# A two-layer attention trunk: the softmax weights transposed by block transposes on VectorE and DMAs through DRAM instead of by TensorE

## The chip, the cores and the metric

The kernel runs on one core of a Trainium2 chip. The metric is the device time of one execution in microseconds (us), as the median of several runs. Single executions were also profiled; all rows below come from one such execution of the kernel before.

## The reference

The reference takes 256 tokens of width 2048 through two layers. Each layer normalises its input (RMSNorm), projects it by one wide matrix to queries, keys, values and a gate, applies rotary embedding to queries and keys, does attention per head, multiplies by silu(gate), projects back and adds the result to the input. A last RMSNorm ends it. Everything is float32.

```
layer 0:  ya = dilated attention, 8 heads of 128   (three windows merge into one softmax with a fixed mask)
          yb = (softmax(q1 k1') - lam * softmax(q2 k2')) v,  4 heads with v of width 256
          x  = x + (concat(ya, rmsnorm(yb)) * silu(z)) @ w_out
layer 1:  yc = causal softmax attention, 16 heads of 128  (one block of 256 keys, so no block choice remains)
          x  = x + (yc * silu(z)) @ w_out
out = rmsnorm(x)
```

Scores are causal: query tokens 0 to 127 see keys 0 to 127, query tokens 128 to 255 see all 256 keys. So a head's softmax weights are three blocks of 128 x 128.

## The kernel before

**Precision.** Float32 products are made of two parts: a high part rounded to the type `float32r`, and a low part, the rest. A product is high x high + high x low + low x high (`mm3`). ScalarE writes the high part as a copy, VectorE subtracts it from the source for the low part.

**Weights.** The weights stream through SBUF in pieces of 128 x 2048 (1 MB, tile `raw`, three buffers, issued by SyncE). Each piece is split in two halves of 128 x 1024 by `split`: ScalarE writes `wh` (L133), VectorE writes `wl` (L134). There are four buffers of `wh` and `wl`, and `split` is called three halves ahead of use.

**Slots.** The main loop walks over slots. A slot is half of one 128 x 1024 split, and two slots use up one split. Weights come in chunks: for each layer four groups g, each with q, k, z (two chunks of 8 slots each) and v (16 slots; group 0 has v first), then four output chunks of 16 slots. In a slot of a q, k or z chunk TensorE does four pairs of matmuls, one with `wh` against the high and low input (L529, 512 columns) and one with `wl` against the high input (L531, 256 columns). After a slot's matmuls the loop calls what `at(slot, f, ...)` has put down for it. Layer 1 begins at slot 320, its output chunks at slot 576.

**Attention.** When the second k chunk of a group has ended, at slot `nxt`, the attention of the group is put down slot by slot. In groups 0 and 1 of layer 0 and in all groups of layer 1 there are four heads h:

- `attn_s` at `nxt + 1 + 3h`: scores by TensorE (`softmax`, tile `ps_s`), masked maximum by VectorE, exponential by ScalarE, scaling by VectorE; the result is tile `p`, 128 x 384, the three blocks side by side, query by key.
- `attn_t` at `nxt + 6 + 3h`: three TensorE transposes of `p` into PSUM (`ps_t`, L352), then the split of the transposed weights: `th` (ScalarE, L357) and `tl` (VectorE, L358), both for the first two blocks, and `t` (ScalarE, L362), a plain copy of the third.
- `attn_o` at `base + 2 + 2h`, `base` being `nxt + 16` for g = 0 and `nxt + 32` otherwise: the product with v (`po`; three matmuls in `mm3`, two with `t`), and `finish_y`, which multiplies by the gate `u` and splits the result (`y`, `yh`, `yl`).

Groups 2 and 3 of layer 0 hold two differential heads each: `diff_s` twice a head, `attn_t` with all three blocks split (`both`), `diff_o` at `nxt + 34 + 5h` (with a square root on GpSimd, tile `rb`, L201), `diff_y` at `nxt + 38 + 5h`.

**Order.** Every engine works through its instructions in a fixed order. The order on each engine is not that of the program text: a planner goes through the program with costs of its own and places an instruction on its engine once, by its account, its inputs and its buffer are there, with the earlier written ones first. It also sets all semaphores. SyncE issues the weights and the outputs, ScalarE the load `gf`, GpSimd no DMA; GpSimd has six small `pow` operations of `rsqrt_mean` and two at the end.

Of the kernel before, what the change touches and what calls it, by code (L numbers as in the profile page):

```python
# [8 lines left out]
F32 = mybir.dt.float32  # L9
F32R = mybir.dt.float32r  # L10
AF = mybir.ActivationFunctionType
# [4 lines left out]
P = 128  # L16
S = 256
# [38 lines left out]
def trunk(ctx, tc, x_nat, x_t, w0, o0, w1, o1, g0, g1, gfin, lam, subln, cos_t, sin_t,  # L56
          mask_d, mask_c, ident_in, out):
    nc = tc.nc
# [8 lines left out]
    work = ctx.enter_context(tc.tile_pool(name="work", bufs=1))  # L67
    small = ctx.enter_context(tc.tile_pool(name="small", bufs=1))
    pacc = ctx.enter_context(tc.tile_pool(name="pacc", bufs=2, space=PSUM))
    patt = ctx.enter_context(tc.tile_pool(name="patt", bufs=1, space=PSUM))  # L70


    chunks = [(kind, layer, g, j, w) for layer in range(2) for kind, g, j, w in layer_chunks()]
# [37 lines left out]
    def split(m):  # L111
        if m >= 2 * NR:
            return
        load(m // 2)
        r = raws[m // 2][:, 2 * (m % 2) * CW:2 * (m % 2 + 1) * CW]
        last = m - 2 * NR + 8
        if 0 <= last < 4:
            h = [xhl[2 * last + i].rearrange("p a b -> p (a b)") for i in range(2)]
            lo = [xhl[8 + 2 * last + i].rearrange("p a b -> p (a b)") for i in range(2)]
        else:  # L120
            ht = wpool.tile([P, 2 * CW], F32R, tag="wh", name=f"wh{m}")
            lt = wpool.tile([P, 2 * CW], F32R, tag="wl", name=f"wl{m}")
            w = wide[m // 2]
            h, lo = ([t[:, i:i + w] for i in range(0, 2 * CW, w)] for t in (ht, lt))
        if m < 2 or 0 <= last < 4:
            for i in range(2):
                if m == 0:
                    split_x(0, i, xr(i))
                rr = r[:, i * CW:(i + 1) * CW]
                nc.scalar.activation(h[i], rr, AF.Copy)  # L130
                nc.vector.tensor_sub(lo[i], rr, h[i].bitcast(F32))
        else:
            nc.scalar.activation(ht, r, AF.Copy)  # L133
            nc.vector.tensor_sub(lt, r, ht.bitcast(F32))  # L134
        splits[m] = (h, lo)
# [18 lines left out]
    def xr(kt):  # L154
        return xraw[kt // 4][:, kt % 4]
# [3 lines left out]
    def split_x(layer, kt, src):  # L159
        g = g_sb[:, layer, kt:kt + 1]  # L160
        h, lo = xhl[kt][:, 0], xhl[kt][:, 1]
        x_ins.append(nc.scalar.activation(h, src, AF.Copy, scale=g).ins)
        nc.vector.scalar_tensor_tensor(lo, src, g, h.bitcast(F32), op0=ALU.mult, op1=ALU.subtract)
# [6 lines left out]
    ident = const.tile([P, P], F32, name="ident")  # L170
# [85 lines left out]
    def at(slot, f, *a):  # L256
        fill.setdefault(slot, []).append((f, a))
# [52 lines left out]
    def mm3(out_, lh, ll, rh, rl, start=True, stop=True):  # L310
        for i, (l, r) in enumerate(((lh, rh), (lh, rl), (ll, rh))):
            nc.tensor.matmul(out_, l, r, start=start and i == 0, stop=stop and i == 2)  # L312

    def softmax(layer, g, h, mask):
        (q, qh, ql), (k, kh, kl) = Q[layer, g], K[layer, g]
        ps = patt.tile([P, 3 * P], F32, tag="S", name="ps_s", bufs=2)
        nc.tensor.matmul(ps[:, 0:P], q[:, h, 0:P], k[:, h, 0:P], start=True, stop=True)  # L317
        mm3(ps[:, P:3 * P], qh[:, h], ql[:, h], kh[:, h], kl[:, h])
        st = small.tile([P, 3, 2], F32, tag="st", name="st", bufs=4)
        p = work.tile([P, 3 * P], F32, tag="p", name="p", bufs=3)  # L320
        for i, sl in enumerate((slice(0, P), slice(P, 3 * P))):
            nc.vector.tensor_tensor_reduce(out=p[:, sl], in0=ps[:, sl], in1=mask[:, sl], scale=-SCALE,  # L322
                                           scalar=3.0e38, op0=ALU.add, op1=ALU.min,
                                           accum_out=st[:, 0, i:i + 1])
        for i, sl in enumerate((slice(0, P), slice(P, 3 * P))):
            nc.scalar.activation(p[:, sl], p[:, sl], AF.Exp, bias=st[:, 0, i:i + 1], scale=-1.0,  # L326
                                 accum_out=st[:, 1, i:i + 1])
        nc.vector.reciprocal(st[:, 2], st[:, 1])
        return p, st
# [16 lines left out]
                                               op0=ALU.mult, op1=ALU.add)  # L346
            box["p"] = p

    def attn_t(box, both=False):
        pt = patt.tile([P, 3 * P], F32, tag="T", name="ps_t")  # L350
        for i in range(3):
            nc.tensor.transpose(pt[:, i * P:(i + 1) * P], box["p"][:, i * P:(i + 1) * P], ident)  # L352

        n = 3 * P if both else S
        th = work.tile([P, n], F32R, tag="th", name="th", bufs=4)
        tl = work.tile([P, n], F32R, tag="tl", name="tl", bufs=4)
        nc.scalar.activation(th, pt[:, 0:n], AF.Copy)  # L357
        nc.vector.tensor_sub(tl, pt[:, 0:n], th.bitcast(F32))  # L358
        t = None
        if not both:  # L360
            t = work.tile([P, P], F32, tag="t", name="t", bufs=4)
            nc.scalar.activation(t, pt[:, n:3 * P], AF.Copy)  # L362
        box["t"] = (t, th, tl)

    def y_tiles():
# [139 lines left out]
    for (kind, layer, g, j, w), slot0 in list(zip(chunks, starts))[:-1]:  # L505
        ps = pacc.tile([P, 2, CW], F32, tag="acc", name=f"acc{slot0}")
        per = CW // w
        nxt = slot0 + KT // per
        for slot in range(slot0, nxt):
            if slot % 2 == 0:  # L510
                split(slot // 2 + AHEAD)
                load((slot // 2 + AHEAD) // 2 + 1)
            if layer == 0 and slot < KT and 2 * AHEAD <= slot + 4 < KT:
                split_x(0, slot + 4, xr(slot + 4))
            wh, wl = splits[slot // 2]
            for i in range(per):
                kt = (slot - slot0) * per + i
                ww = (slot % 2) * per + i
                first, final = kt == 0, kt == KT - 1
                for b in range(2):  # L520
                    bs = slice(b * P, (b + 1) * P)
                    if w == CW:
                        a_h, a_l = (yh[kt][:, bs], yl[kt][:, bs]) if kind == "o" else \
                            (xhl[kt][:, 0, bs], xhl[kt][:, 1, bs])
                        mm3(ps[:, b], a_h, a_l, wh[ww], wl[ww], start=first, stop=final)
                    else:

                        xx = xhl[kt].rearrange("p a b -> p (a b)")
                        nc.tensor.matmul(ps[:, b], wh[ww][:, bs], xx, start=first, stop=False,  # L529
                                         skip_group_check=True)  # L530
                        nc.tensor.matmul(ps[:, b, 0:S], wl[ww][:, bs], xx[:, 0:S], start=False, stop=final,  # L531
                                         skip_group_check=True)
            for f, a in fill.pop(slot, []):
                f(*a)
        if kind == "z":
            evac_z(ps, layer, g, j)
        elif kind == "q":
            evac_rope(ps, "q", Q, layer, g, j)
        elif kind == "k":
            evac_rope(ps, "k", K, layer, g, j)  # L540
            if j == 0:
                continue
            if layer == 0 and g >= 2:
                for h in range(2):
                    box = {}
                    at(nxt + 1 + 6 * h, diff_s, layer, g, h, box, 0)
                    at(nxt + 3 + 6 * h, diff_s, layer, g, h, box, 1)
                    at(nxt + 8 + 6 * h, attn_t, box, True)
                    at(nxt + 34 + 5 * h, diff_o, layer, g, h, box)
                    at(nxt + 38 + 5 * h, diff_y, layer, g, h, box)  # L550
            else:
                for h in range(4):
                    box = {}
                    base = nxt + (16 if g == 0 else 32)
                    at(nxt + 1 + 3 * h, attn_s, layer, g, h, md if layer == 0 else mc, box)
                    at(nxt + 6 + 3 * h, attn_t, box)
                    at(base + 2 + 2 * h, attn_o, layer, g, h, box)
        elif kind == "v":
            if slot0 == 0:
                at(nxt + 5, evac_v, ps, layer, g)  # L560
            else:
                evac_v(ps, layer, g)
        else:
            evac_o(ps, layer, g)
            if layer == 0:
                at(nxt + 3, next_x, g, 0)
                at(nxt + 6, next_x, g, 1)
            else:
                at(nxt + 4, times_g, g)
# [65 lines left out]
```

## Time and profile before

| | us |
|---|---|
| median of 3 runs | 958.21 (958.12 to 958.51) |
| profiled execution, its own time | 958.89 |
| its span, first to last instruction | 957.1 |
| TensorE matmuls busy | 946.3 |
| VectorE busy | 639.3 |
| ScalarE busy | 526.3 |
| GpSimd busy | 6.0 |

The mean granted TensorE clock is 0.996 of full speed. The DMAs move 177.09 MB, 185 GB/s in the mean. In the profile PE is TensorE, PEld its weight loads, DVE is VectorE, ACT is ScalarE, POOL is GpSimd and SP is SyncE; a q behind a name is the engine's sequencer or DMA queue. L352 is line 352 of the kernel. An engine's idle time costs something only where it delays what comes last.

### The profile page before, as it was taken

The page shows a single profiled execution, that of the slowest core. Times are in us where ns is not written, and L with a number is a line of the kernel's source. Part 1 is how long each engine was busy: PE and PEld are TensorE (multiplying, and loading weights), DVE is VectorE, ACT ScalarE, POOL GpSimd, SP SyncE. Part 2 cuts the span into 40 slices and gives each one's busy share as a digit, 9 for nine tenths or more (in the row PEclk, how much of TensorE's full clock was granted, in tenths as well). Part 3 has the DMA queues.
Part 4 walks back from the last instruction along what each step waited for, and adds up shares of the span by engine and source line. Part 5 has one row for each costly group of instructions (what it writes and reads, how often), then busy time and mean ns, then how long its engine had stood idle before and what let it go on. Part 6 is the DMA issues. An engine that isn't in the chain of part 4 may idle for free.

```text
span 957.1 us, 13108 instructions
## 1 busy us (share of the span) xinstructions
PE 946.3 (99%) x5132; PEld 819.1 (86%) x5132; DVE 639.3 (67%) x973; ACT 526.3 (55%) x807; POOL 6.0 (1%) x12
## 2 busy tenths in 40 slices
PE   8999999999999999999999999999999999999996
PEld 7888888888888888888888898888889888888886
DVE  6778678557856785655566787685678567755572
ACT  7556556445645564454544665564566455644451
POOL 0000000000000000000000000000000000000000
PEclk9999999999999999999999999999999999999999
DMA  9775454445554554544555544545454545554542
GB/s 327 247 295 181 146 190 176 169 175 195 185 173 162 196 179 175 176 176 176 181 176 203 190 169 156 203 155 194 164 191 170 182 173 180 191 205 176 181 171 88
DMA packets 27854, 177.09 MB, mean 185 GB/s; under 512 B 3344, under 2 KB 4112, under 8 KB 7696
## 3 DMA queue, kind: packets, MB, share of 16 engines
q1 hardware_dynamic: 27504, 175.21, 51.5%
q10 hardware_dynamic: 288, 1.05, 0.4%
q8 instruction: 40, 0.66, 0.3%
q14 instruction: 22, 0.18, 0.1%
HBM read 174.15 MB, written 2.10 MB: 184 GB/s over the span
## 4 chain that ended last, share of the span: by engine, by line
PE 96%; issue 1%; DMA 1%; SPq 0%; ACT 0%; DVE 0%; POOL 0%; POOLq 0%; ACTq 0%
PE acc L529 36%; PE acc L312 34%; PE acc L531 19%; PE ps_s L312 1%; PE last L462 1%; PE ps_t L352 1%; DMA raw<-in_w 1%; PE po L312 1%; PE ps_s L317 1%; PE po L383 1%; PE pdo L312 0%; PE ps_xt L426 0%; PE ps_yt L409 0%; SPq L99 0%; SPq L150 0%
## 5 line engine op out<-in xcount | busy, mean ns | idle before, releaser
L134 DVE TENSOR_TENSOR wl<-raw,wh 128x1024 fp32r<-128x1024 f32 x314 | 384.3, 1224 | 244.7 <-ACT wh L133 242.2
L529 PE MATMUL acc<-x,wh 128*128 128x512 f32 x1536 | 541.1, 393 | 0.0
L133 ACT ACTIVATE wh<-raw 128x1024 fp32r<-128x1024 f32 x314 | 332.3, 1059 | 292.5 <-PE acc L529 138.4
L531 PE MATMUL acc<-x,wl 128*128 128x256 f32 x1536 | 432.8, 282 | 0.0
L529 PEld LDWEIGHTS acc<-x,wh 128*128 128x128 f32 x1536 | 288.5, 188 | 58.4
L531 PEld LDWEIGHTS acc<-x,wl 128*128 128x128 f32 x1536 | 290.2, 189 | 0.3
L312 PE MATMUL acc<-wh,x 128*128 128x512 f32 x512 | 164.8, 400 | 1.6 <-ACT wh L130 1.6
L312 PEld LDWEIGHTS acc<-wh,x 128*128 128x128 f32 x512 | 96.9, 189 | 24.8 <-ACT wh L130 1.8
L312 PE MATMUL acc<-wl,x 128*128 128x512 f32 x256 | 101.9, 398 | 0.5 <-DVE wl L134 0.2
L312 PE MATMUL acc<-wh,yh 128*128 128x512 f32 x224 | 88.4, 394 | 0.0
L312 PE MATMUL acc<-wh,yl 128*128 128x512 f32 x224 | 87.3, 390 | 0.0
L312 PE MATMUL acc<-wl,yh 128*128 128x512 f32 x224 | 87.2, 389 | 0.0
L312 PEld LDWEIGHTS acc<-wl,x 128*128 128x128 f32 x256 | 48.5, 190 | 12.6 <-DVE wl L134 0.7
L312 PEld LDWEIGHTS acc<-wh,yl 128*128 128x128 f32 x224 | 42.0, 188 | 9.0
L312 PEld LDWEIGHTS acc<-wl,yh 128*128 128x128 f32 x224 | 42.1, 188 | 8.3
L312 PEld LDWEIGHTS acc<-wh,yh 128*128 128x128 f32 x224 | 42.1, 188 | 8.3
L326 ACT ACTIVATE p<-p,st 128x128 f32<-128x128 f32 x64 | 28.5, 448 | 9.9 <-DVE st L322 9.6
L375 ACT ACTIVATE yh<-y 128x256 fp32r<-128x256 f32 x32 | 13.0, 417 | 34.4 <-DVE y L374 34.3
L290 DVE TENSOR_TENSOR rt<-rt,sr 128x512 f32<-128x512 f32 x32 | 22.1, 690 | 3.7 <-ACT rt L288 2.4
L287 ACT ACTIVATE rt<-rt 64x512 f32<-64x512 f32 x32 | 20.2, 631 | 7.7 <-DVE rt L286 7.0
L286 DVE TENSOR_TENSOR rt<-acc,rt 128x512 f32<-128x512 f32 x32 | 21.8, 683 | 0.1
L288 ACT ACTIVATE rt<-rt 64x512 f32<-64x512 f32 x32 | 20.2, 632 | 0.4
(131 smaller groups left out, 646.9 us busy)
## 6 DMA issues: line engine op xcount, KB each, us to landing
raw<-in_w SPq DMA_DIRECT2D x124, 1024.0 KB, 4.7
raw<-in_o SPq DMA_DIRECT2D x32, 1024.0 KB, 4.7
raw<-in_w SPq DMA_DIRECT2D x7, 512.0 KB, 8.7
xraw<-in_x_t SPq DMA_DIRECT2D x8, 256.0 KB, 7.7
x_sb<-in_x_nat SPq DMA_DIRECT2D x1, 2048.0 KB, 11.0
out<-x_sb SPq DMA_DIRECT2D x8, 256.0 KB, 2.5
gf<-in_gfin ACTq DMA_DIRECT2D x2, 512.0 KB, 4.5
raw<-in_w SPq DMA_DIRECT2D x2, 256.0 KB, 4.5
```

The lines of the kernel that those rows point to most:

```text
L133: nc.scalar.activation(ht, r, AF.Copy)
L134: nc.vector.tensor_sub(lt, r, ht.bitcast(F32))
L286: nc.vector.tensor_add(t1, ps[:, :, 0:S], t1)
L287: nc.scalar.activation(t2[0:64], t1[64:128], AF.Copy)
L288: nc.scalar.activation(t2[64:128], t1[0:64], AF.Copy)
L290: nc.vector.tensor_mul(t2, t2, sr[:, None, :].to_broadcast([P, 2, S]))
L312: nc.tensor.matmul(out_, l, r, start=start and i == 0, stop=stop and i == 2)
L317: nc.tensor.matmul(ps[:, 0:P], q[:, h, 0:P], k[:, h, 0:P], start=True, stop=True)
L326: nc.scalar.activation(p[:, sl], p[:, sl], AF.Exp, bias=st[:, 0, i:i + 1], scale=-1.0, accum_out=st[:, 1, i:i + 1])
L375: nc.scalar.activation(yh[kt], y, AF.Copy)
L529: nc.tensor.matmul(ps[:, b], wh[ww][:, bs], xx, start=first, stop=False, skip_group_check=True)
L531: nc.tensor.matmul(ps[:, b, 0:S], wl[ww][:, bs], xx[:, 0:S], start=False, stop=final, skip_group_check=True)
```

## The change

`attn_t` no longer uses TensorE. VectorE transposes `p` within each block of 32 x 32 (12 blocks along each group of 32 partitions) into a tile `bt`. One DMA issued by GpSimd stores `bt` to a DRAM tile `d`, and four more bring it back into `p`, one for each 32 partitions of the result, so that rows of blocks and columns of blocks change places. Each row of `p` then holds, for one key, the queries in runs of 32. A new function `attn_h` splits the result into `th`, `tl` and `t` where the head is soon multiplied by v. `p` gets five buffers instead of three; `th`, `tl` and `t` two instead of four. `attn_t` is put down two slots earlier, `attn_h` two slots ahead of `attn_o`, and for g = 0 `base` is six slots later.

```diff
+    dram = ctx.enter_context(tc.tile_pool(name="dram", bufs=2, space=bass.MemoryType.DRAM))
...
-        p = work.tile([P, 3 * P], F32, tag="p", name="p", bufs=3)
+        p = work.tile([P, 3 * P], F32, tag="p", name="p", bufs=5)
...
-    def attn_t(box, both=False):
-        pt = patt.tile([P, 3 * P], F32, tag="T", name="ps_t")
-        for i in range(3):
-            nc.tensor.transpose(pt[:, i * P:(i + 1) * P], box["p"][:, i * P:(i + 1) * P], ident)
-
-        n = 3 * P if both else S
-        th = work.tile([P, n], F32R, tag="th", name="th", bufs=4)
-        tl = work.tile([P, n], F32R, tag="tl", name="tl", bufs=4)
-        nc.scalar.activation(th, pt[:, 0:n], AF.Copy)
-        nc.vector.tensor_sub(tl, pt[:, 0:n], th.bitcast(F32))
+    def attn_t(box):
+        p = box["p"]
+        bt = work.tile([P, 4, 3, 32], F32, tag="bt", name="bt", bufs=2)
+        nc.vector.transpose(bt.rearrange("p c b j -> p b c j"), p.rearrange("p (b c j) -> p b c j", b=3, c=4))
+        d = dram.tile([P, 4, 3 * 32], F32, tag="d", name="d")
+        nc.gpsimd.dma_start(d, bt.rearrange("p c b j -> p c (b j)"))
+        pt = p.rearrange("p (a x) -> p a x", a=4)
+        dv = d.rearrange("(a i) c x -> c i a x", a=4)
+        for c in range(4):
+            nc.gpsimd.dma_start(pt[32 * c:32 * c + 32], dv[c])
+
+    def attn_h(box, both=False):
+        n = 3 if both else 2
+        pt = box["p"].rearrange("p (a b j) -> p b a j", a=4, b=3)
+        th = work.tile([P, n * P], F32R, tag="th", name="th", bufs=2)
+        tl = work.tile([P, n * P], F32R, tag="tl", name="tl", bufs=2)
+        th4, tl4 = (t.rearrange("p (b a j) -> p b a j", b=n, a=4) for t in (th, tl))
+        nc.scalar.activation(th4, pt[:, 0:n], AF.Copy)
+        nc.vector.tensor_sub(tl4, pt[:, 0:n], th4.bitcast(F32))
         t = None
         if not both:
-            t = work.tile([P, P], F32, tag="t", name="t", bufs=4)
-            nc.scalar.activation(t, pt[:, n:3 * P], AF.Copy)
+            t = work.tile([P, P], F32, tag="t", name="t", bufs=2)
+            nc.scalar.activation(t.rearrange("p (a j) -> p a j", a=4), pt[:, 2], AF.Copy)
         box["t"] = (t, th, tl)
...
-                    at(nxt + 8 + 6 * h, attn_t, box, True)
+                    at(nxt + 6 + 6 * h, attn_t, box)
+                    at(nxt + 32 + 5 * h, attn_h, box, True)
...
-                    base = nxt + (16 if g == 0 else 32)
+                    base = nxt + (22 if g == 0 else 32)
...
-                    at(nxt + 6 + 3 * h, attn_t, box)
+                    at(nxt + 4 + 3 * h, attn_t, box)
+                    at(base + 2 * h, attn_h, box)
```

## Rows read from the trace of the kernel before

**Rows 1.** Page, part 1: busy us, share of the span, instructions of each engine.
```profile
PE 946.3 (99%) x5132; PEld 819.1 (86%) x5132; DVE 639.3 (67%) x973; ACT 526.3 (55%) x807; POOL 6.0 (1%) x12
```

**Rows 2.** TensorE's waits, first and last of four: waited for, us, times, longest.
```profile
PE acc L312 <- ACT wh L130: 1.6, 1, 1.6
...
PE acc L312 <- DVE wl L131: 0.2, 1, 0.2
```

**Rows 3.** Chain of waits around three stretches of attention: start us, us, what.
```profile
84.70 0.22 PE ps_s L317 x2
84.92 0.35 PE ps_s L312 x3
...
87.71 0.23 PE acc L529
87.94 0.12 PE acc L531
88.05 0.33 PE ps_t L352 x3
88.38 0.23 PE acc L529
...
836.51 0.33 PE ps_t L352 x3
...
873.33 0.35 PE po L312 x3
```

**Rows 4.** Groups by shape: line, engine, operation | busy us, mean ns | idle before, releaser.
```profile
L134 DVE TENSOR_TENSOR wl<-raw,wh 128x1024 fp32r<-128x1024 f32 x314 | 384.3, 1224 | 244.7 <-ACT wh L133 242.2
...
L376 DVE TENSOR_TENSOR yl<-y,yh 128x256 fp32r<-128x256 f32 x32 | 13.2, 423 | 9.5 <-ACT yh L375 9.3
...
L358 DVE TENSOR_TENSOR tl<-ps_t,th 128x256 fp32r<-128x256 f32 x24 | 9.9, 411 | 0.0
L357 ACT ACTIVATE th<-ps_t 128x256 fp32r<-128x256 f32 x24 | 9.0, 376 | 0.6
...
L334 DVE TENSOR_SCALAR p<-p,st 128x256 f32<-128x256 f32 x24 | 8.3, 347 | 0.0
...
L362 ACT ACTIVATE t<-ps_t 128x128 f32<-128x128 f32 x24 | 6.7, 278 | 23.4 <-DVE tl L358 23.4
...
L358 DVE TENSOR_TENSOR tl<-ps_t,th 128x384 fp32r<-128x384 f32 x4 | 2.2, 552 | 0.1
```

**Rows 5.** Two full stretches: busy PE, PEld, DVE, ACT, POOL (count), clock, DMA share, GB/s.
```profile
150.00:172.00 22.00, 22.00 (x139) 19.81 (x138) 18.08 (x44) 15.48 (x34) 0.00 (x0) 1.00 0.44 156
243.00:265.00 22.00, 22.00 (x137) 19.75 (x136) 18.95 (x46) 14.74 (x30) 0.00 (x0) 1.00 0.52 188
```

**Rows 6.** Issue on SyncE, GpSimd's `rb`: count, ns least/median/most, first and last start, shapes.
```profile
L106 SPq DMA_DIRECT2D raw<-in_w x124: 327/328/332, 17.0 to 833.6; - x124
...
L201 POOL TENSOR_TENSOR rb<-v,half x4: 691/692/702, 298.7 to 402.5; 128x2 f32<-128x2 f32 x4
```

**Rows 7.** DMA issues: line, engine, count, KB each, us from issue to landing.
```profile
out<-x_sb SPq DMA_DIRECT2D x8, 256.0 KB, 2.5
gf<-in_gfin ACTq DMA_DIRECT2D x2, 512.0 KB, 4.5
...
cosT<-in_cos_t SPq DMA_DIRECT2D x1, 128.0 KB, 6.0
```

**Rows 8.** ScalarE in order of time: start us, us, line, operation, [idle before, releaser].
```profile
124.78 1.06 ACT L133 ACTIVATE wh<-raw 128x1024 fp32r<-128x1024 f32 x1 [1.67 <-issue]
127.57 1.06 ACT L133 ACTIVATE wh<-raw 128x1024 fp32r<-128x1024 f32 x1 [1.72 <-PE acc L529]
...
828.91 0.38 ACTq L435 DMA_DIRECT2D gf<-in_gfin  x1
```

## The prediction

> **What bounds the kernel now.** I read the page's busy table first: TensorE is busy for 946.3 of 957.1 us, VectorE for two thirds, ScalarE for about half, GpSimd for 6 us [rows 1]. TensorE's own list of waits comes next: four waits, about 3 us in all, none during the attention [rows 2]. So the order and length of TensorE's instructions set the end, and I go to the chain of waits around one call of `attn_t` [rows 3]. There an accumulating pair of matmuls (L529, L531) takes 0.35 us, four pairs make a slot of 1.39 us, and three transposes stand between two pairs as one piece of 0.33 us. The next pair starts right behind it. What the path pays for a call is this 0.33 us.
>
> **The change part by part.**
>
> *Transposes leave TensorE.* `attn_t` runs 28 times: 8 heads in layer 0's groups 0 and 1, 4 pairs in groups 2 and 3, 16 heads in layer 1. The chain has 28 pieces `PE ps_t L352 x3`, each 0.33 us; the first and the last are shown [rows 3]. 28 x 0.33 = 9.24 us come off the path. The first pairs behind a transpose are some hundredths longer than the others, so up to 0.5 us more may go.
>
> *VectorE gets 28 block transposes of 128x384.* No such instruction is in the trace. Below is the 0.35 us of a 128x256 `tensor_scalar`, above the 1.22 us of a 128x1024 subtraction; I take 0.55 us, the row for 128x384 elements [rows 4]. In the fullest stretch with four heads VectorE is busy for 18.08 of 22 us, with a differential pair of heads 18.95 [rows 5]. Four transposes add 2.2 us to the one, and three to four subtractions of 0.41 us (`tl`) leave it for later; two add 1.1 us to the other, and one or two of 0.55 us leave it. Both stay near 19 us, or 21.5 us at the upper end (four more times 1.22 us, less 1.6 us): no cost to TensorE, since `wl` is written ahead. If this cover went, 28 x 0.55 = 15 us would show.
>
> *The split moves (`attn_h`).* `th`, `tl` and `t` now read SBUF instead of PSUM. The SBUF-to-SBUF subtraction of 128x256 (L376) takes 423 ns against 411 ns, so it costs nothing more [rows 4]. With two buffers instead of four, head 2's `th` waits until head 0's `attn_o` is done. It then has two `attn_o` distances, about 6.7 us (two slots and some 0.57 us of `po` matmuls each), for 1.07 us of work (0.38, 0.41 and 0.28 us, rows 4). For g = 0 `attn_o` moves by six slots. It is the same TensorE work, its `u` is overwritten only at the end of the next group's first z chunk, 56 slots after this k chunk, and nothing waits for `yh` there.
>
> *Five DMAs a head on GpSimd.* One store of 192 KB, then, after it has landed, four loads of 48 KB. Behind a waiting GpSimd instruction stand only the DMAs of later heads; its `rb` work comes over 20 slots later. Let x be the time that GpSimd needs to issue one. The lowest bound is SyncE's issue, 0.33 us; GpSimd's nearest row is 0.69 us for a tiny operation, and I take 0.7 us [rows 6]. The store lands in 2.5 us by the nearest row, the output store. For the loads I take 4.5 us, that of `gf`, the one load on a queue without weights; the queue with weights gives 6.0 us for a small one [rows 7]. So the first head is back 5x + 7 = 10.5 us after its block transpose. Heads come every 4.75 us (three slots and 0.57 us of score matmuls, 0.22 and 0.35 us in rows 3), and GpSimd is held for 5x + 2.5 = 6.0 us by each. If GpSimd keeps to one head after the other, the fourth is back after 5x + 7 + 3 x (5x + 2.5 - 4.75) = 20x + 0.25 = 14.3 us. Its room from written `attn_t` to `attn_o` is 17 slots and three earlier heads' `po`, 25.3 us, less 1.2 us for the split: 24 us for g = 0. In the other groups of four heads it is 27 slots, 38 us, and in the differential groups 28 and 27 slots for two heads. Cost on the path: nothing, up to x = 1.19 us. With all bounds at their upper ends (0.7 us; 6.0 us for store and loads alike) the fourth is back after 5 x 0.7 + 12 + 3 x (9.5 - 4.75) = 29.8 us, 5.8 us late in two groups: 11.6 us.
>
> The Trainium skill (SBUF — State Buffer, "SBUF: two separate sides") says that a DMA issued by GpSimd needs its cores to write descriptors, that these can't be written while VectorE runs an operation in a mode that uses the shared port pair, and that one transfer took about 3.1 us instead of 0.62 us beside one. No run here shows a GpSimd DMA. The sum by its figure stands with the first rival.
>
> *The weight stream.* 28 x 0.39 MB add 11 MB to 177 MB. The 16 DMA engines are busy for 44 and 52% in those stretches [rows 5], so I cost this at nothing.
>
> *Sum.* 957.1 - 9.24 = 947.9 us of span. The profiled execution took 958.89 us, 1.8 us more than its span, so 949.65 us by that. It lies 0.68 us above the median of the runs, 958.21 us, from which 9.24 us gives **949.0 us**. The likeliest case's own range is 948.4 to 951 us: the longer pairs below, a fourth head late by about 1 us in each of the two tight groups above.
>
> **The rivals.**
>
> *A. GpSimd issues too slowly; slower.* The place is `attn_o` of the fourth head. TensorE waits when 20x + 0.25 exceeds 24 us (two groups) or 38 us (four groups). The gain is used up at 2 x (20x + 0.25 - 24) = 9.24, x = 1.42 us. At x = 1.5 us two groups lose 6.25 us each, giving 961.5 us; at 2 us the loss is 2 x 16.25 + 4 x 2.25 = 41.5 us, 990 us. If GpSimd could issue only while VectorE is idle, 3.92 of 22 us [rows 5], x would be 0.7 x 22 / 3.92 = 3.9 us, and the loss 2 x 54 + 4 x 40 = 268 us, 1217 us. For it speaks that VectorE is so busy and that no row bounds x above. Against it: only a small part of VectorE's work there is `tensor_scalar` (0.35 us for 256 elements against 0.42 us for the two-input form, rows 4), and the room is large. Chance 0.12, of which 0.03 for issuing beside an idle VectorE alone. By the Trainium skill's figure x would be near 3.1 us, and 20x + 0.25 = 62 us would lose about 172 us, an estimate from that page. The Trainium skill (same page, "Who interferes with whom") also infers that operations with two SBUF inputs, the bulk here, don't stop descriptor writing; no run here shows either.
>
> *B. ScalarE stands in front of data that is not there; slower.* Instructions don't wait for their written slot. The `gf` DMA is written after slot 588, four slots behind the last group's last `po` at 873.33 us, but ScalarE issued it at 828.91 us, when its buffer came free [rows 3, 8]. So the planner may put `th` of the first heads as soon as it believes the loads have landed. If they land later, ScalarE waits, and the next `wh` behind it. How long that is free shows in the splits: two slots are 2.79 us apart, a `wh` starts when TensorE leaves its buffer [rows 8], three splits before it is used, 8.4 us, and 2.3 us of it go to `wh` and `wl` themselves. 6.1 us are covered, nearer 5 with other work between. Each us beyond is paid in up to 8 groups; 9.24 / 8 = 1.15 us a group uses up the gain. 3 us beyond the cover give 949 + 24 = 973 us. With nothing allowed for by the planner the first head would be 10.5 - 6.1 = 4.4 us beyond, 984 us. For it: the four loads come after a store and are the longest path that anything here waits for. Against it: any plausible allowance above 5 us closes the gap. Chance 0.13.
>
> *C. The same two mechanisms, but small.* One to two us late in some groups, 2 to 7 us in all: 951 to 956 us. Chance 0.15. The gain just used up: 0.05.
>
> **How the numbers follow.** Forecast 0.55, C 0.15, used up 0.05, A 0.12, B 0.13. 0.2% is about what a measurement of this kernel can tell from no change, 1.9 us. Faster 0.70, same 0.05, slower 0.25. For the range I leave out the far part of A and B, some 0.17, and the little below the forecast's lower end: 947.8 to 963 us.
>
> **What would show it.** Right: no `ps_t` piece in the chain; a VectorE row of 28 transposes near 0.5 us; TensorE's waits still about 3 us; GpSimd issues below 1.2 us each; ScalarE's `th` either not waiting or by less than 5 us. Rival A shows as `po` waiting for `th` or `tl` in g = 0 first, with GpSimd's queue busy from the first `attn_t` to the fourth `attn_o`. Rival B shows as ScalarE waiting for a DMA ahead of `th` and TensorE's `acc` matmuls waiting for `wh` soon after. A TensorE idle time that grows by more than 9 us makes the prediction wrong in sign; a gain above 11 us would show that the path paid more for the transposes than the chain says.

## The result, and the profile after

The changed kernel takes 949.40 us (949.34 to 949.67, 4 runs) where the kernel before took 958.34 us in the same comparison: a ratio of 0.9907, 95% interval 0.989 to 0.9925. The forecast was 949.0 us. The profiled execution took 949.46 us, its span is 947.7 us, 9.4 us less than the 957.1 us of before.

The page's first part, which answers to [rows 1]:

```profile
PE 936.5 (99%) x5048; PEld 809.1 (85%) x5048; DVE 651.7 (69%) x1001; ACT 527.0 (56%) x807; POOL 82.9 (9%) x152
```

TensorE has 84 matmuls fewer (5132 to 5048) and is still busy for 99% of the span. VectorE has 28 instructions and 12.4 us more, GpSimd 140 and 77 us more. ScalarE has as many as before. TensorE's whole list of waits, which answers to [rows 2] (what was waited for, us in all, times, longest):

```profile
PE pw L149 <- DVE fs L463: 1.1, 1, 1.1
PE acc L313 <- ACT wh L131: 0.9, 1, 0.9
PE acc L313 <- DVE wl L135: 0.8, 1, 0.8
PE acc L313 <- DVE wl L132: 0.4, 2, 0.2
```

It is 3.2 us, about 3 us as before, all at the start and at the warm-up matmuls. Nothing in the attention makes TensorE wait.

The instructions of the new path, from the views of the tiles `bt`, `d` and `th` (count, then least, median and longest ns; start of the first and last in us; shapes):

```profile
L355 DVE STREAM_TRANSPOSE bt<-p x28: 569/574/580, 85.8 to 827.0; 128x384 f32<-128x384 f32 x28
L357 POOL DMA_DIRECT2D d<-bt x28: 557/561/733, 86.7 to 830.2; - x28
...
L361 POOL DMA_DIRECT2D p<-d x112: 548/548/638, 91.3 to 838.2; - x112
...
L371 DVE TENSOR_TENSOR tl<-p,th x28: 412/417/559, 98.4 to 858.2; 128x256 fp32r<-128x256 f32 x24, 128x384 fp32r<-128x384 f32 x4
```

The block transpose takes 0.574 us, an issue on GpSimd about 0.55 us, and `tl` out of SBUF takes what it took out of PSUM [rows 4]. The DMA issues by line (count, KB each, us from issue to landing) answer to [rows 7]:

```profile
raw<-in_w SPq DMA_DIRECT2D x124, 1024.0 KB, 4.8
...
d<-bt POOLq DMA_DIRECT2D x28, 192.0 KB, 4.7
p<-d POOLq DMA_DIRECT2D x112, 48.0 KB, 3.7
```

The same two stretches as in [rows 5]:

```profile
150.00:172.00 22.00, 22.00 (x136) 19.73 (x135) 18.17 (x47) 13.72 (x30) 5.83 (x11) 1.00 0.56 184
243.00:265.00 22.00, 22.00 (x135) 19.73 (x135) 20.51 (x49) 14.59 (x30) 3.31 (x6) 1.00 0.50 168
```

TensorE is busy without a gap. VectorE stands at 18.17 us in the stretch with four heads, and at 20.51 us in the one with two differential heads. The first figure looks lower than it is: only 6.44 us of `wl` fall into that stretch, where it was 8.56 us before.

GpSimd in order of time, the first group of heads (start us, us, operation, how often; idle time before it and what ended it):

```profile
86.69 0.73 POOL L357 DMA_DIRECT2D d<-bt  x1 [46.48 <-DVE st L323]
91.27 2.18 POOL L361 DMA_DIRECT2D p<-d  x4 [3.84 <-DMA d<-bt]
93.44 1.24 POOL L357 DMA_DIRECT2D d<-bt  x2
98.38 4.36 POOL L361 DMA_DIRECT2D p<-d  x8 [3.71 <-DMA d<-bt]
...
109.81 2.17 POOL L361 DMA_DIRECT2D p<-d  x4 [6.52 <-DMA d<-bt]
```

The planner issues the stores of heads 1 and 2 together and then their eight loads, so two landings overlap. The store of the fourth head comes behind them. Its last load is issued by 111.98 us, 11 us after its block transpose ended (100.88 us), and lands at 116.9 us. ScalarE's wait for what `th` reads (us in all, times, longest):

```profile
ACT th L370 <- DMA p<-d: 30.6, 12, 5.1
```

ScalarE stands before `th` for 30.6 us in all, 5.1 us at most. None of it reaches TensorE.

### The profile page after: what moved, and what is told of

Its sections match the earlier page's. It is cut to its first block, busy times and chain, and to the rows that moved or that the text cites. A ratio compares the mean times of both kernels' runs of the same rounds, so it can differ in the third digit from the quotient of the medians.

```text
span 947.7 us, 13307 instructions
## 1 busy us (share of the span) xinstructions
PE 936.5 (99%) x5048; PEld 809.1 (85%) x5048; DVE 651.7 (69%) x1001; ACT 527.0 (56%) x807; POOL 82.9 (9%) x152
## 4 chain that ended last, share of the span: by engine, by line
PE 96%; issue 1%; DMA 1%; SPq 0%; ACT 0%; DVE 0%; POOL 0%; POOLq 0%; ACTq 0%
PE acc L542 37%; PE acc L313 34%; PE acc L544 19%; PE ps_s L313 1%; PE last L475 1%; PE po L313 1%; DMA raw<-in_w 1%; PE ps_s L318 1%; PE po L396 1%; PE pdo L313 0%; PE ps_xt L439 0%; PE ps_yt L422 0%; SPq L100 0%; SPq L151 0%; DVE wl L135 0%
## 5 line engine op out<-in xcount | busy, mean ns | idle before, releaser
L361 POOL DMA_DIRECT2D p<-d x112 | 61.1, 552 | 104.4 <-DMA d<-bt 53.8
L357 POOL DMA_DIRECT2D d<-bt x28 | 15.9, 569 | 471.6 <-DVE st L323 348.2
L370 ACT ACTIVATE th<-p 128x256 fp32r<-128x256 f32 (+1 forms) x28 | 12.1, 431 | 36.8 <-DMA p<-d 30.6
```

Source lines behind the costliest of these rows:

```text
L357: nc.gpsimd.dma_start(d, bt.rearrange("p c b j -> p c (b j)"))
L361: nc.gpsimd.dma_start(pt[32 * c:32 * c + 32], dv[c])
L370: nc.scalar.activation(th4, pt[:, 0:n], AF.Copy)
```

## The experiments

Every experiment was timed in turns with the kernel before, whose median in these comparisons was 958.35 to 958.53 us. What is not named in an edit is as in the changed kernel.

**1. TensorE's transposes put back, without their use.**

```diff
+    def dead_t():
+        dead = patt.tile([P, 3 * P], F32, tag="T", name="ps_dead")
+        for i in range(3):
+            nc.tensor.transpose(dead[:, i * P:(i + 1) * P], ident, ident)
...
+                    at(nxt + 8 + 6 * h, dead_t)
...
+                    at(nxt + 6 + 3 * h, dead_t)
```

> The changed kernel with three TensorE transposes of the identity put back at the slots where the kernel before had its transposes; their result is read by nobody, the data still takes the new path. Theory (the whole gain is the 28 pieces of 0.33 us on TensorE): 949.4 + 9.24 = 958.6 us, within 1 us of the kernel before. Rival (part of the gain comes from the splits, which now read SBUF at another time): between 950 and 957 us.

Measured: 958.61 us, a ratio to the kernel before of 1.0004 (0.9995 to 1.0014). In its chain of waits the piece is back, and two calls of the scores stand 5.08 us apart (84.21 to 89.29 us):

```profile
84.21 0.22 PE ps_s L318 x2
...
87.56 0.33 PE ps_dead L366 x3
...
89.29 0.22 PE ps_s L318 x2
```

In the chain of the changed kernel they stand 4.74 us apart:

```profile
84.36 0.22 PE ps_s L318 x2
...
89.10 0.22 PE ps_s L318 x2
```

The 28 pieces are the whole gain. The rival falls: moved splits, buffers and the path itself give and take nothing that this comparison can tell (its interval is about 1 us wide to either side).

**2. The room for group 0 taken back.**

```diff
-                    base = nxt + (22 if g == 0 else 32)
+                    base = nxt + (16 if g == 0 else 32)
```

> The changed kernel with attn_o of group 0 at its old slots, six slots (8.4 us) earlier. By the trace of the changed kernel the last load of head 3 is issued at 111.98 us and lands some 4 us later; with 0.8 us for th and tl the fourth po could start at about 116.9 us, and would be wanted at 123.9 - 8.4 = 115.5 us. Theory (the room between attn_t and attn_o decides): TensorE waits some 1.4 us for th or tl in two groups, 952 us, 950.5 to 955. Rival (the moved slots do nothing, there is room to spare): 949.4 us, with no TensorE wait on th or tl.

Measured: 951.01 us (950.08 to 954.11), ratio 0.9927 (0.991 to 0.9944). The longest entry of TensorE's list of waits is now one for `th`, and the chain of waits shows where it comes from:

```profile
PE po L313 <- ACT th L370: 1.7, 1, 1.7
```

```profile
102.10 6.33 DMA d<-bt
...
110.60 5.84 DMA p<-d
...
116.55 0.42 ACT th L370
...
117.02 0.39 PE po L313
```

The chain leaves TensorE, runs through the fourth head's store, GpSimd's issues, the load and `th`, and comes back at 117.02 us, as the expectation had it (116.9 us). The six slots are needed: they hide the round trip in the tight group. The expectation had TensorE wait in both groups with g = 0; its list has the one wait of 1.7 us, in layer 0, and none for `th` or `tl` in layer 1. The loss is 1.6 us and not 2.6.

**3. ScalarE no longer standing before loads.**

```diff
-            nc.scalar.activation(ht, r, AF.Copy)
+            last_wh[:] = [nc.scalar.activation(ht, r, AF.Copy).ins]
...
+        with tc.issue_after(last_wh[0]):
             nc.scalar.activation(th4, pt[:, 0:n], AF.Copy)
```

The copy `t` is held in the same way.

> The changed kernel with th and t held behind the last wh written before them, so that ScalarE does not stand in front of loads on their way. In the changed kernel it stood there for 30.6 us in 12 waits, the longest 5.1 us. Theory (these waits are covered by the splits that are ready ahead, some 5 to 6 us): they vanish from ScalarE's list and the time stays 949.4 us, within 0.7 us. Rival (they cost part of the gain now): 946 to 948 us. Second rival (th now comes too late for the first po of a group): 951 us or more, with TensorE waiting for th or tl.

Measured: 949.41 us (948.8 to 949.54). The waits of `th` are gone from ScalarE's list, and the time is the same: 30.6 us of waits cost nothing.

**4. The weight splits held back until the first head is split.**

```diff
-                    at(nxt + 32 + 5 * h, attn_h, box, True)
+                    at(nxt + (32 + 5 * h if h else 6), attn_h, box, True, h == 0)
...
-                    at(base + 2 * h, attn_h, box)
+                    at(base + 2 * h if h else nxt + 4, attn_h, box, False, h == 0)
...
+            with (tc.issue_after(hold.pop()) if hold else nullcontext()):
                 nc.scalar.activation(ht, r, AF.Copy)
```

`hold` keeps the `th` of a group's first head, so the next `wh` comes behind it.

> The changed kernel with the split of each group's first head written right behind its attn_t and the next wh held behind that th, so that ScalarE does no weight split until the first head's data are back. In the changed kernel bt is done at 86.3 and th runs at 98.0 us; the held wh would normally start at about 86.3 us and is used at about 95.8 us. It would now end at 99.5 us and its wl at 100.7 us. Theory (rival B of the prediction: standing costs what exceeds the cover, one to one): TensorE waits 3 to 5 us in each of 8 groups for wh or wl, 949.4 + 24 to 40 = 973 to 990 us. Rival (the splits ready ahead cover this too): below 953 us.

Measured: 971.97 us, ratio 1.0142 (1.0126 to 1.0157). The cost is 22.6 us, a little under the range: the first head's `th` ran at 95.20 us, not at 98.0. Its loads had landed at 94.7 us, not at 97.9, because the held split also puts off the next weight load, from 91.58 us in the changed kernel to 99.31 us here, and no weight load was under way beside them (experiment 6 comes back to this). In these first two groups `th` has no wait for a load; it stands behind the fourth head's exponential, and `wh` behind `th`. So these groups do not show ScalarE standing before a load. They show what the prediction says follows from that: no `wh` runs for 12.2 us (83.53 to 95.71 us), and TensorE runs dry. ScalarE in the first group, and then TensorE in the second:

```profile
95.20 0.40 ACT L372 ACTIVATE th<-p 128x256 fp32r<-128x256 f32 x1
...
95.71 3.89 ACT L136 ACTIVATE wh<-raw 128x1024 fp32r<-128x1024 f32 x4
```

```profile
168.03 0.39 PE L546 MATMUL acc<-x,wh 128*128 128x512 f32 x1
...
168.37 0.39 PE L546 MATMUL acc<-x,wh 128*128 128x512 f32 x1
...
170.35 0.50 PE L546 MATMUL acc<-x,wh 128*128 128x512 f32 x1 [1.48 <-ACT wh L136]
171.75 0.39 PE L548 MATMUL acc<-x,wl 128*128 128x256 f32 x1 [0.90 <-DVE wl L137]
...
172.32 0.62 PE L546 MATMUL acc<-x,wh 128*128 128x512 f32 x1
...
172.96 0.63 PE L546 MATMUL acc<-x,wh 128*128 128x512 f32 x1
```

Four weight splits stand in a row behind `th`. TensorE waits 1.48 us for `wh` and 0.90 us for `wl`. From 172.3 us on a pair takes 0.64 us (172.32 to 172.96), not the 0.34 us of before the wait (168.03 to 168.37), until 175.5 us. The granted clock before the waits, in the 5 us behind them, and in the slow stretch alone (columns as in [rows 5]):

```profile
165.00:170.00 5.00, 3.88 (x25) 3.25 (x23) 3.36 (x13) 2.61 (x8) 3.39 (x7) 1.00 0.37 118
170.00:175.00 5.00, 3.75 (x13) 3.01 (x14) 4.99 (x5) 3.15 (x4) 4.16 (x8) 0.73 0.47 95
172.30:175.50 3.20, 3.20 (x12) 2.72 (x11) 2.80 (x3) 0.84 (x1) 1.86 (x4) 0.50 0.62 147
```

It falls from 1.00 to 0.50, that is from 2.4 to 1.2 GHz, after TensorE had stood. So a wait costs more than its length: of the 21.6 us by which the span grew, TensorE idles for 12.6 us, and the same matmuls are busy for 9.0 us more (945.5 against 936.5 us). The mean granted clock, 0.992 against 0.998, accounts, by an estimate, for 969.3 x 0.008 - 947.7 x 0.002 = 5.9 us of those 9.0; the rest isn't told apart.

**5. Each load cut into four.**

```diff
-            nc.gpsimd.dma_start(pt[32 * c:32 * c + 32], dv[c])
+            for a in range(4):
+                nc.gpsimd.dma_start(pt[32 * c:32 * c + 32, a], dv[c][:, a])
```

> The changed kernel with each of the four loads of a head cut into four (17 DMAs a head instead of 5; the same bytes). GpSimd's issue of a load takes 0.55 us in the changed kernel's trace, so a head holds it 12 x 0.55 = 6.6 us longer and the fourth head is back 26.4 us later: at about 142 us instead of 116 us in the first group, where th has to be done by about 123 us, and at 214 us instead of 188 us in the second, where po stands at 209 us. Theory (rival A of the prediction: GpSimd's issue time times the number of DMAs, against the room): TensorE waits some 19 us in two groups and 5 to 6 us in four, 949.4 + 58 to 63 = about 1010 us, 990 to 1025. Rival (the DMAs' landing bounds, not the issue): below 960 us.

Measured: 1023.96 us (1012.44 to 1027.48), ratio 1.0663 (1.06 to 1.0727). GpSimd takes 0.50 us for each small load and is busy for 241.8 us. ScalarE's longest wait for loads, and the page's row on the engines:

```profile
ACT th L371 <- DMA p<-d: 99.3, 16, 8.8
```

```profile
PE 960.9 (94%) x5048; PEld 825.7 (81%) x5048; DVE 650.4 (64%) x1001; ACT 523.4 (51%) x807; POOL 241.8 (24%) x488
```

The rival, that landing bounds, falls: the landings are no longer than in the changed kernel (3.8 us for the store, 3.5 us for a load), and the time is far above 960 us. The loss of 74.6 us to the changed kernel is above the 58 to 63 us of the sum. The profile divides it: of the 76.0 us by which the span grew (1023.7 us), TensorE idles for 51.6 us, a little under the sum, and the same matmuls are busy for 24.4 us more, at a mean granted clock of 0.971 instead of 0.998, which the sum left out. The room is thus real, and five DMAs a head lie well within it.

**6. The same DMAs issued by SyncE.**

```diff
-        nc.gpsimd.dma_start(d, bt.rearrange("p c b j -> p c (b j)"))
+        nc.sync.dma_start(d, bt.rearrange("p c b j -> p c (b j)"))
...
-            nc.gpsimd.dma_start(pt[32 * c:32 * c + 32], dv[c])
+            nc.sync.dma_start(pt[32 * c:32 * c + 32], dv[c])
```

> The changed kernel with the same five DMAs a head issued by SyncE, behind and between the weight loads, instead of by GpSimd. Theory (issue and landing are covered, whoever issues): 949.4 us, within 1 us; an issue takes 0.33 us instead of 0.55 us. Rival 1 (SyncE stands before a load until the store has landed, and weight loads behind it come late): 953 us or more, with ScalarE's wh waiting for raw. Rival 2 (VectorE keeps GpSimd from writing its descriptors): a store lands in about 2.5 us here instead of 4.7 us, and ScalarE's waits for p shrink; by the landing of the weight loads in the same queue (4.7 us) I expect 4 us or more here too.

Measured: 951.61 us (951.46 to 951.77), ratio 0.9929 (0.9914 to 0.9944). My expectation missed twice, on the time and on the landing. The landings, and ScalarE's wait for weights:

```profile
d<-bt SPq DMA_DIRECT2D x28, 192.0 KB, 2.5
p<-d SPq DMA_DIRECT2D x112, 48.0 KB, 2.4
```

```profile
ACT wh L134 <- DMA raw<-in_w: 14.5, 8, 3.5
```

A store lands in 2.5 us and a load in 2.4 us, against 4.7 and 3.7 us from GpSimd, and ScalarE no longer waits for `p`. That is the sign that the expectation gave for rival 2, but the traces give it another cause: what decides is whether a weight load is under way beside the DMA. The first store of the first group starts 1.1 to 1.4 us behind a weight load in both kernels; the first store of the third group starts 0.6 to 0.9 us before one has landed. GpSimd, then SyncE, in each (columns as in [rows 7]):

```profile
d<-bt POOLq DMA_DIRECT2D x1, 192.0 KB, 4.3
...
d<-bt SPq DMA_DIRECT2D x1, 192.0 KB, 4.8
```

```profile
d<-bt POOLq DMA_DIRECT2D x1, 192.0 KB, 2.1
...
d<-bt SPq DMA_DIRECT2D x1, 192.0 KB, 1.8
```

Over all loads of `p`, sorted by whether a weight load is under way for at least 1 us of the first 2 us, the medians are 4.35 us (GpSimd, 83 of 112) and 4.33 us (SyncE, 58 of 112) beside one, 2.13 and 1.97 us otherwise. So the issuing engine makes a difference of 0.2 to 0.3 us where no weight load is in the way, and not the 1.3 to 2.2 us of the medians over all. SyncE's DMAs meet fewer weight loads because SyncE, while it stands before the loads of `p` and issues them, issues no weight load: after the one at 85.17 us the next comes only at 99.85 us.

```profile
91.08 3.89 SPq L361 DMA_DIRECT2D p<-d  x8
...
99.85 0.35 SPq L107 DMA_DIRECT2D raw<-in_w  x1
```

The changed kernel issues that weight load at 91.58 us. The path lands sooner, and yet the kernel is slower by 2.2 us. That is the direction of rival 1, a little under its 953 us, but not by the waits that it names. Those for `raw`, 14.5 us in all (0.7 us in the changed kernel), lie at 182.8 us and later and don't reach TensorE. Matmul by matmul TensorE falls behind the changed kernel by 1.1 us in each of the two groups with g = 0, and by next to nothing elsewhere. There no `wh` runs for 10.7 us, since the planner put `rt` and the heads' splits in front of the next ones, and `wl` comes late once in each group:

```profile
105.60 2.12 ACT L134 ACTIVATE wh<-raw 128x1024 fp32r<-128x1024 f32 x2
112.33 0.60 ACT L286 ACTIVATE rt<-acc 128x512 f32<-128x512 f32 x1 [4.61 <-PE acc L544]
...
118.42 1.99 ACT L134 ACTIVATE wh<-raw 128x1024 fp32r<-128x1024 f32 x2
```

```profile
PE acc L544 <- DVE wl L135: 0.6, 2, 0.3
```

Whether the planner did so because it reckoned with late weight loads is likely, and not shown.

**7. More transposes off TensorE: x between the layers.** `next_t` transposes the 128x512 halves of a finished output chunk on VectorE, stores 512 KB and loads it back in eight DMAs; `next_h` splits it. The last chunk keeps TensorE, since layer 1 needs it at once. The edits of experiment 3 are in it.

```diff
-            if layer == 0:
+            if layer == 0 and g < 3:
+                box = {}
+                at(nxt + 1, next_t, g, box)
+                for k in range(4):
+                    at(nxt + 12 + k, next_h, g, k, box)
+            elif layer == 0:
                 at(nxt + 3, next_x, g, 0)
```

> The changed kernel with th and t held as in the run before that held them, and with the transposes of x between the layers taken off TensorE in the same way for three of the four output chunks (two VectorE transposes of 128x512, one store and eight loads of 64 KB a chunk; the split nine slots later, held behind the last wh). The chain has eight pieces of 0.44 us for them; six go. Theory: 949.4 - 2.64 = 946.8 us, 946.3 to 947.5. Rival (x is late for layer 1 or for the next chunk): no gain, with ScalarE or TensorE waiting for xt.

Measured: 952.73 us (950.68 to 956.2), slower than the changed kernel. ScalarE in order of time, and TensorE's first wait:

```profile
467.83 1.06 ACT L135 ACTIVATE wh<-raw 128x1024 fp32r<-128x1024 f32 x1 [1.66 <-PE acc L314]
477.28 0.91 ACT L465 ACTIVATE x<-xt,g_sb 128x256 fp32r<-128x256 f32 x2 [8.38 <-DMA xt<-dx]
```

```profile
PE ps_xt L442 <- DVE x_sb L433: 3.3, 2, 3.0
```

The loads were issued by 471 us and landed at 477 us. ScalarE stood for 8.38 us; VectorE's evacuation of the last chunk stood behind it, and TensorE's remaining transposes waited for that, 3.0 us at once. Here too the granted clock fell behind the wait, to 0.78 between 480 and 485 us. A wait of 5.95 us for the chunk before, until 453.08 us, left no wait on TensorE's list.

**8. The same, with the split five slots later.**

```diff
-                    at(nxt + 12 + k, next_h, g, k, box)
+                    at(nxt + 17 + k, next_h, g, k, box)
```

Two tiles take other buffers, since one chunk's data now live on beside the next one's; the run does not part that from the slots.

> As the run that took six of the eight transposes of x off TensorE, but with the splits of x written five slots later (17 to 20 slots behind the end of the chunk instead of 12 to 15), so that ScalarE does not stand before loads that have not landed: there it stood for 8.4 us from 468.9 us, past the splits that are ready ahead, and VectorE's evacuation behind it came 3 us late for TensorE. Theory (the place of the split cost the gain, not the path): 949.4 - 6 x 0.44 = 946.8 us, 946.2 to 947.6, no ScalarE wait of over 3 us on xt. Rival (the path itself costs, by its 512 KB stores and loads beside the weights): 949.4 us or more.

Measured: 946.77 us (946.41 to 946.94), ratio 0.9877 (0.9861 to 0.9894), as worked out. Its runs lie 2.4 us below the lowest of the changed kernel, and 1.9 us below the lowest of experiment 3, whose edits it has. No wait for `xt` is among ScalarE's, and TensorE waits for 3.4 us in all, 1.1 us at most, none of it for `ps_xt`.

## Why the prediction was right

*The term that carries the sum held.* The path paid 28 x 0.33 us for the transposes; experiment 1 gives 958.61 - 949.40 = 9.2 us for them, the forecast 9.24 us. Reading the 0.33 us off the chain, not from the duration of single matmuls, made the size right.

*VectorE.* 0.55 us was taken for a block transpose, 0.574 us measured, 16.1 us in all. The forecast of 19 us for the stretch with differential heads was low: 20.51 us. One `tl` was to leave it and is in it as before (0.52 and 0.54 us), and 0.3 us more of `wl` fall into it. It was covered all the same.

*GpSimd.* An issue takes 0.55 us, not 0.7. The store's landing was mis-sized: 2.5 us taken from the output store, 4.7 us measured. The nearest row misled because the output stores run from 941 us on, when the last weight load has landed; beside one, a DMA waits (experiment 6). The prediction cost the weight stream at nothing, and that holds for the weights, not for what runs beside them. By the sum as it was written, 20 x 0.55 + 4 x 4.7 + 3.7 - 14.25 = 19.3 us, the fourth head would still have been within the 24 us. It was back 16.0 us after its block transpose (100.88 to 116.9 us), since GpSimd did not keep to one head after the other and the stores of two heads landed side by side. That this lies near the forecast 14.3 us is partly luck: an issue put 0.15 us too high, an order that saved time and a landing put 2.2 us too low offset each other. The room was wide enough for either, and experiment 2 shows that it was not idle: six slots less cost 1.6 us.

*Rival A* was the right place. Experiment 5 drives GpSimd past the room and loses 74.6 us. At x = 0.55 us the kernel is on the safe side of the 1.19 us from which the prediction let it cost; with the landing as measured the same sum reaches 24 us at x = (24 + 14.25 - 18.8 - 3.7) / 20 = 0.79 us, so the margin was smaller than written. The Trainium skill's 3.1 us for a transfer held up by VectorE (SBUF — State Buffer, "SBUF: two separate sides") does not show in the issues, the longest of which is 0.73 us, and the landings follow the weight loads: a load that meets none lands in 2.1 us, beside a VectorE that is busy for 3.94 of 4.72 us (98.38 to 103.10 us).

*Rival B* was half of what happened: `th` was planned before its data, and ScalarE stood 30.6 us. It cost nothing because no wait was longer than 5.1 us against a cover put at 5 to 6 us. Experiment 3 shows that the waits are free. How near the edge was shows in the longest time without a `wh`: 6.9 us in the changed kernel (819.20 to 826.11 us), free; 10.7 us in experiment 6, which cost 1.1 us a group; 12.2 us in the groups of four heads of experiment 4 (11.8 to 12.7 us), which cost more. That standing before a load itself does harm when it is long enough shows most plainly in experiment 7, and there through VectorE's evacuation, not through `wh`. This was close; the forecast gave it 0.13, and nothing in the trace of before could have told where the planner would put `th`.

*The weight stream* was not disturbed: 4.8 us to landing against 4.7 us.

## What to carry to other kernels

On a kernel whose bound engine never waits, work taken off that engine is worth what the chain of waits says, and a round trip through DRAM is free as long as its result is wanted later than it can be back. Work out the two rooms separately: from start to use for the bound engine, and for every engine that waits in order, how long it may stand before the bound engine runs dry. Put the consumer's instruction where the data surely are, and issue such a round trip from a queue behind which nothing urgent stands. Size its landing by a DMA that runs beside the same traffic, not by one that runs alone.

## What the runs showed of the hardware that was not expected

- A small DMA that starts beside a 1 MB weight load lands later, whoever issues it: a load of 48 KB took 4.35 us in the median beside one and 2.13 us otherwise (GpSimd), 4.33 and 1.97 us (SyncE). The Trainium skill (DMA: Bandwidth & Descriptors, "Latency and other measured facts") puts about 0.4 us between the two issuers to the first byte; the landings without a weight load, 2.13 against 1.97 us, show no more than that.
- After TensorE had stood for 1.48 and 0.90 us with one matmul between, its matmuls ran for some 3 us at about half the pace (0.64 us a pair instead of 0.34), with a granted clock of 0.50 there: 1.2 GHz instead of 2.4. Over experiment 4, 12.6 us of idle time cost 21.6 us of span.
- VectorE's transpose of 32x32 blocks of 4-byte values took 0.574 us for 128x384, with a strided output, much like a subtraction of that size (0.552 us, rows 4).
